# A tuned skewness kernel rewritten as one hand-synchronised section: x in a ring of two blocks, the transposes in a loop on PE, one ACT sum in every block

## The chip, the cores and the metric

The kernel runs on one core of one Trainium2 chip. The metric is the device time in microseconds (us), as a median of several executions. The engines are called as in the profile: PE (matmuls), PEld (PE's weight loads, which lie beside its matmuls), DVE (vector), ACT (scalar), POOL (GpSimd), SP (SyncE, which here issues every load). Blocks, loads and pieces are numbered from 0, so the eight blocks are 0 to 7. "b2" is block 2.

## The reference

The input is 1024 rows of 8192 float32 values (33.5 MB); the output is the skewness of each row.

```python
mean = np.mean(x, axis=-1, keepdims=True)
std = np.std(x, axis=-1, keepdims=True)
z = (x - mean) / (std + 1e-8)
return np.mean(z ** 3, axis=-1)
```

## The kernel before

The rows lie in eight blocks of 128. Of each piece of a block, ACT makes the squares (and their sum), DVE multiplies the squares by x (and sums the cubes), and PE sums x itself: it transposes 128 columns at a time and lets the transposes add up in `tp`. ACT copies `tp` to SBUF, a small matmul by 1/n gives the mean, and a few small instructions close the block. Only in blocks 0 to 2 does ACT take 1024 columns of the plain sum off PE.

```python
UNITS = [                       # columns of each load, block by block
    [4096, 4096], [4096, 4096], [4096, 4096], [4096, 4096],
    [3584, 2304, 2304],
    [2304, 2304, 2048, 1536],
    [1664, 1792, 1920, 1664, 1152],
    [1024, 1024, 1152, 1280, 1408, 1152, 1152],
]
S1_ACT = {(0, 0): 1024, (1, 0): 1024, (2, 0): 1024}
X_BUFS = 8
# ... cut ...
for b, widths in enumerate(UNITS):
    tp = psum.tile([P, P], FP, tag="tp", name=f"tp_{b}")
    for k, w in enumerate(widths):
        xt = xpool.tile([P, w], FP, tag="x", name=f"x_{b}_{k}")
        nc.sync.dma_start(out=xt, in_=xv[b, :, c0 : c0 + w])
        for s, e in _slices(w):
            # ACT: square with sum of squares;  DVE: cube with sum of cubes
            # ... cut ...
        w_act = S1_ACT.get((b, k), 0)
        if w_act:               # ACT: sum of 1024 columns
            # ... cut ...
        for c in range((w - w_act) // P):
            nc.tensor.matmul(out=tp, lhsT=xt[:, c * P : (c + 1) * P], rhs=ident,
                             start=..., stop=..., is_transpose=True)
    nc.scalar.copy(out=tsb, in_=tp)
    nc.tensor.matmul(out=s1ps[:, b : b + 1], lhsT=tsb, rhs=onesn, start=True, stop=True)
```

A scheduling layer places the buffers and semaphores. Each PE instruction waits for the load that it reads.

## Time and profile before

| | before |
|---|---|
| time, median of 4 executions beside the changed kernel | 91.49 us (91.40 to 91.57) |
| span of the profiled execution | 89.7 us |
| busy: DVE, ACT, PE | 72.7, 72.1, 64.9 us |
| mean granted clock of PE | 0.978 |
| last landing of x | 83.56 us |

The span runs from the first to the last record of the profile; the time contains 1.8 us more. The prediction below shows the chain, the DMA strips and the end. Two more views of before matter for what came. The first is the view of waits. Each line names an engine, the tile and line that waited, what it waited for, then the total in us, the number of waits, and the longest.

```profile
PE tp L165 <- DMA x<-in_x_dram: 17.2, 14, 8.2
DVE sq L152 <- ACT sq L147: 13.3, 7, 9.2
...
ACT sq L147 <- DMA x<-in_x_dram: 9.9, 8, 6.0
...
ACT tsb L174 <- PE tp L165: 2.0, 2, 1.5
```

Everybody waits for x, ACT too: eight times, 5.95 us of it for the first load. ACT waits for PE's transposes at the copy into `tsb` only twice. The second is the strips of the page (the profile's summary): busy tenths and granted clock in 40 slices.

```profile
PE   0003999892882919989998988888987798969710
...
ACT  6003999699991999859898989978979898999950
...
PEclk9999999999999997599999999999999999999998
```

PE's clock falls once before the end, in slices 15 and 16, to half (34.6 to 38.0 us). There, 32 transposes take 5.38 us; ACT's copy waits 1.48 us for them, and nothing comes of it: at 43.61 us ACT waits for a load again.

### The profile page before, as it was taken

What the parts mean: (1) busy time and instruction counts of PE and PEld (TensorE: products, weight loads), DVE (VectorE), ACT (ScalarE), POOL (GpSimd) and SP (SyncE); (2) the same over time, 40 slices, a digit from 0 to 9 for tenths busy, and PEclk for the clock granted to TensorE, in tenths of its full rate; (3) what the DMA queues carried; (4) which work ended last, traced back from release to release, by engine and by line L of the source; (5) the groups of instructions that cost most, each with busy time, mean ns of one, the idle gap of its engine ahead of it and who ended that gap; (6) DMA issues with size and microseconds to landing.
All of it is one profiled execution on the core that took longest, in us unless ns stands there. A gap on an engine that the chain in (4) does not pass through costs nothing.

```text
span 89.7 us, 1368 instructions
## 1 busy us (share of the span) xinstructions
PE 64.9 (72%) x504; PEld 59.3 (66%) x504; DVE 72.7 (81%) x80; ACT 72.1 (80%) x106; POOL 11.3 (13%) x14
## 2 busy tenths in 40 slices
PE   0003999892882919989998988888987798969710
PEld 0003999791872909979897977877876787848500
DVE  1000498989999298995999999999999999999970
ACT  6003999699991999859898989978979898999950
POOL 3000000000000000000000000000005999900030
PEclk9999999999999997599999999999999999999998
DMA  3999999999999999999999999999999999994000
GB/s 117 351 424 438 424 431 431 431 431 424 446 416 431 424 438 424 424 438 427 415 409 418 419 427 419 421 415 419 409 414 417 404 413 411 421 412 161 0 0 2
DMA packets 4038, 33.64 MB, mean 375 GB/s; under 512 B 576, under 2 KB 576, under 8 KB 2240
## 3 DMA queue, kind: packets, MB, share of 16 engines
q1 hardware_dynamic: 4032, 33.56, 89.7%
q8 instruction: 4, 0.07, 0.3%
q14 instruction: 2, 0.02, 0.0%
HBM read 33.55 MB, written 0.00 MB: 374 GB/s over the span
## 4 chain that ended last, share of the span: by engine, by line
DMA 73%; ACT 13%; issue 5%; DVE 4%; SPq 1%; PE 1%; DVEq 0%; ACTq 0%
DMA x<-in_x_dram 73%; ACT sq L147 9%; DVE sq L152 3%; ACT sqps L147 1%; ACT same L159 1%; SPq L140 1%; PE s1ps L175 1%; ACT tsb L174 0%; ACT s3u L128 0%; ACT v L127 0%; ACT var L125 0%; DVE num L189 0%; ACT m1sq L124 0%; DVE skew L192 0%; ACT nm L126 0%
## 5 line engine op out<-in xcount | busy, mean ns | idle before, releaser
L152 DVE SCALAR_TENSOR_TENSOR sq<-sq,x 128x2048 f32<-128x2048 f32 (+9 forms) x35 | 70.7, 2071 | 13.4 <-ACT sq L147 13.3
L165 PE MATMUL tp<-ident,x 128*128 128x128 f32 x488 | 62.6, 288 | 17.3 <-DMA x<-in_x_dram 17.2
L165 PEld LDWEIGHTS tp<-ident,x 128*128 128x128 f32 x488 | 57.9, 150 | 20.9 <-DMA x<-in_x_dram 12.7
L147 ACT ACTIVATE sq<-x 128x2048 f32<-128x2048 f32 (+9 forms) x35 | 60.6, 1734 | 10.7 <-DMA x<-in_x_dram 9.9
L110 POOL TENSOR_TENSOR vara<-m2a,m1sqa 128x6 f32<-128x6 f32 x1 | 1.8, 1822 | 67.1 <-DVE m3a L99 67.1
L147 ACT ACTIVATION_READ_ACCUMULATOR sq<-x 128x1 f32 x35 | 6.5, 186 | 0.0
L175 PEld LDWEIGHTS s1ps<-onesn,tsb 128*128 128x128 f32 x16 | 2.4, 188 | 5.2 <-ACT tsb L174 5.2
L175 PE MATMUL s1ps<-onesn,tsb 128*128 128x1 f32 x16 | 3.1, 260 | 3.3 <-ACT tsb L174 3.3
L174 ACT COPY tsb<-tp 128x128 f32<-128x128 f32 x8 | 2.0, 256 | 2.0 <-PE tp L165 2.0
L114 POOL TENSOR_TENSOR rra<-vara,expo 128x6 f32<-128x6 f32 x1 | 3.3, 3267 | 0.0
L159 ACT ACTIVATE same<-x 128x1024 f32<-128x1024 f32 x3 | 3.1, 1041 | 0.0
L152 DVE DVE_READ_ACCUMULATOR sq<-sq,x 128x1 f32 x35 | 2.9, 83 | 0.0
L111 POOL TENSOR_TENSOR m1sq3a<-m1sq3a,vara 128x6 f32<-128x6 f32 x1 | 1.9, 1868 | 0.1
L77 ACT ACT_TABLE_LOAD x1 | 1.3, 1283 | 0.7 <-PEq L208 0.7
L187 POOL TENSOR_TENSOR rr<-var,expo 128x2 f32<-128x2 f32 x1 | 0.7, 702 | 7.7 <-ACT var L125 7.7
L152 DVE SCALAR_TENSOR_TENSOR cube<-sqps,x 128x1152 f32<-128x1152 f32 x1 | 1.4, 1350 | 0.0
L113 POOL TENSOR_TENSOR m3a<-m3a,m1sq3a 128x6 f32<-128x6 f32 x1 | 1.2, 1201 | 0.1
L147 ACT ACTIVATE sqps<-x 128x1152 f32<-128x1152 f32 x1 | 1.1, 1136 | 0.1
L115 POOL TENSOR_TENSOR skew<-m3a,rra 128x6 f32<-128x6 f32 x1 | 1.1, 1069 | 0.1
L124 ACT ACTIVATE m1sq<-s1ps 128x1 f32<-128x1 f32 x2 | 0.3, 171 | 0.5 <-PE s1ps L175 0.5
L75 DVE MEMSET onesn<- 128x1 f32 x1 | 0.1, 59 | 0.8 <-PEq L208 0.8
L112 POOL TENSOR_TENSOR m1sq3a<-m1sq3a,nm1a 128x6 f32<-128x6 f32 x1 | 0.7, 697 | 0.0
(28 smaller groups left out, 6.8 us busy)
## 6 DMA issues: line engine op xcount, KB each, us to landing
x<-in_x_dram SPq DMA_DIRECT2D x8, 2048.0 KB, 23.4
x<-in_x_dram SPq DMA_DIRECT2D x4, 1152.0 KB, 27.9
x<-in_x_dram SPq DMA_DIRECT2D x4, 576.0 KB, 8.6
x<-in_x_dram SPq DMA_DIRECT2D x1, 1792.0 KB, 33.0
x<-in_x_dram SPq DMA_DIRECT2D x2, 832.0 KB, 13.9
x<-in_x_dram SPq DMA_DIRECT2D x1, 1024.0 KB, 21.1
x<-in_x_dram SPq DMA_DIRECT2D x2, 512.0 KB, 10.0
x<-in_x_dram SPq DMA_DIRECT2D x1, 960.0 KB, 13.2
```

The costliest lines, as they stand in the source:

```text
L77: nc.scalar.activation(out=tiny, in_=onesn, func=AF.Square)
L110: g.tensor_tensor(out=var, in0=m2, in1=m1sq, op=ALU.subtract)
L111: g.tensor_tensor(out=m1sq3, in0=m1sq3, in1=var, op=ALU.add)
L113: g.tensor_tensor(out=m3, in0=m3, in1=m1sq3, op=ALU.add)
L114: g.tensor_tensor(out=rr, in0=var, in1=expo, op=ALU.pow)
L115: g.tensor_tensor(out=skew[:, 0:F], in0=m3, in1=rr, op=ALU.mult)
L147: nc.scalar.activation(out=sq, in_=xt[:, s:e], func=AF.Square, scale=s_scale, accum_out=s2u[:, j : j + 1],)
L152: nc.vector.scalar_tensor_tensor(out=cube, in0=sq, scalar=1.0, in1=xt[:, s:e], op0=ALU.mult, op1=ALU.mult, accum_out=s3u[:, j : j + 1],)
L159: nc.scalar.activation(out=same[:, 0:w_act], in_=xt[:, w - w_act : w], func=AF.Copy, scale=inv_n, accum_out=s1a[:, b : b + 1],)
L165: nc.tensor.matmul(out=tp, lhsT=xt[:, c * P : (c + 1) * P], rhs=ident, start=(k == 0 and c == 0), stop=(c0 == C and c == n - 1), is_transp ...
L174: nc.scalar.copy(out=tsb, in_=tp)
L175: nc.tensor.matmul(out=s1ps[:, b : b + 1], lhsT=tsb, rhs=onesn, start=True, stop=True)
```

## The change

The intent was to make PE's program small enough (56 transposes a block, two blocks in a loop of four trips) that its instruction packets vanish (before has four of 16 KB on queue 8, 1.02 to 1.09 us each), to halve the memory for x, and to cut the number of loads from 27 to 24. The whole program is now one section whose semaphores are placed by hand. The core of the diff, with cuts at "...":

```diff
-    [3584, 2304, 2304],
-    [2304, 2304, 2048, 1536],
-    [1664, 1792, 1920, 1664, 1152],
-    [1024, 1024, 1152, 1280, 1408, 1152, 1152],
+    [2304, 2944, 2944],
+    [2176, 1664, 2176, 2176],
+    [1920, 2304, 2304, 1664],
+    [1536, 1920, 1792, 1664, 1280],
 ]
-S1_ACT = {(0, 0): 1024, (1, 0): 1024, (2, 0): 1024}
-X_BUFS = 8
+S1_ACT = 1024
+RING = 2
+ISSUE_LAG = 6500
+PARTS = (
+    [2048, 4096, 6144, 7168, 8192],
+    [2048, 4096, 5120, 6144, 7168, 7680, 8192],
+)
 ...
+    ring = sb("ring", RING * C)
 ...
+    ready = []
+    for u, (b, k, s, e) in enumerate(units):
+        free = []
+        if b >= RING:
+            o = b - RING
+            free = [("cube", max(i for i in of_block[o] if slices[i][2] < e)),
+                    ("part", o, min(i for i, p in enumerate(PARTS[o % RING]) if p >= e)),
+                    ("s1a", o)]
+        ready.append((max(b * C + e - RING * C + ISSUE_LAG, 0) if b >= RING else 0, u, 0, free))
+        n = sum(s < p <= e for p in PARTS[b % RING])
+        if n:
+            ready.append((b * C + e + 900, u, n, [("x", u)]))
+    for _, u, n, waits in sorted(ready, key=lambda r: r[:2]):
+        if n:
+            pr.op("sync", ("more", u), waits, lambda n=n: nc.sync.sem_inc(more, n), counts=False)
+        else:
 ...                              # the load of unit u, behind its waits
+    def pe_program(tensor):
+        tensor.wait_ge(*pr.marks["ident"])
+        tensor.wait_ge(*pr.marks["onesn"])
 ...
+        with nc.Fori(0, NB // RING, engines=..., head_slot={only: 0}):
+            for h in range(RING):
+                c0 = S1_ACT
+                for i, end in enumerate(PARTS[h]):
+                    tensor.sem_inc(more, -1)._wait_ge(more, 1)
+                    for c in range(c0, end, P):
+                        t = nc.tensor.matmul(out=tp[h], lhsT=at(h, c, c + P), rhs=ident, ...)
```

The loop's body is the same code in each trip and names no load's own semaphore. So PE waits for one counter, `more`, and SP raises it when a load has landed. SP therefore has one ordered list with two kinds of entries: loads, each behind the waits that free its part of the ring, and releases of PE, each behind the landing that it reports. `ISSUE_LAG` sets where a load stands in that list.

## The prediction

> **What bounds the kernel now.** I read the page's chain of work first, then its strips of 40 slices and its DMA queues.

> ```profile
> DMA 73%; ACT 13%; issue 5%; DVE 4%; SPq 1%; PE 1%; DVEq 0%; ACTq 0%
> ...
> DMA  3999999999999999999999999999999999994000
> GB/s 117 351 424 438 424 431 431 431 431 424 446 416 431 424 438 424 424 438 427 415 409 418 419 427 419 421 415 419 409 414 417 404 413 411 421 412 161 0 0 2
> ...
> q8 instruction: 4, 0.07, 0.3%
> ```

> The load of x is the path: 73% of it, and all 16 DMA engines are at 9 from slice 1 to slice 35. A buffer that frees sooner or a faster DVE cannot move that. But the strip holds an oddity. Slice 36 (80.7 to 82.97 us) moves 161 GB/s, slice 37 nothing, and yet the last square waits for x until 83.56 us. So I asked for the end in short stretches (length, then busy time and count of PE, PEld, DVE, ACT, POOL, then clock, DMA share, GB/s):

> ```profile
> 80.00:81.00 1.00, 0.58 (x6) 0.35 (x5) 1.00 (x1) 1.00 (x3) 0.00 (x0) 1.00 1.07 423
> 81.00:81.50 0.50, 0.50 (x6) 0.50 (x6) 0.50 (x3) 0.50 (x1) 0.00 (x0) 1.00 0.64 258
> 81.50:82.00 0.50, 0.50 (x7) 0.50 (x5) 0.50 (x1) 0.50 (x1) 0.00 (x0) 1.00 0.32 129
> 82.00:82.50 0.50, 0.50 (x5) 0.27 (x4) 0.50 (x3) 0.50 (x3) 0.00 (x0) 1.00 0.18 74
> 82.50:83.00 0.50, 0.50 (x7) 0.50 (x6) 0.50 (x1) 0.50 (x1) 0.00 (x0) 1.00 0.11 46
> ```

> A share of 0.11 is two of sixteen engines. Two stragglers hold the end. In the trace's records of the last load's 16 landings, the median engine is done at 81.89 us and the last two at 83.41 and 83.56. In the first load the spread from median to last is only 0.45 us (7.64 to 8.09). So some 1.2 us of the end is skew that grew on the way. It grew in jumps, each at an instruction packet: queue 8 has 16 KB packets at 26.28, 47.37, 65.24 and 80.88 us, taking 1.02 to 1.09 us each. The load that lands after the first has one engine 1.2 us late (28.85 against a next-to-last 27.65); after the second there are two. PE has issued about 230, 470, 730 and 1000 matmuls and weight loads at these times, so these are PE's instructions[...].[...]

> The tail after the last landing, in order of time (start, duration, engine):

> ```profile
> 83.58 1.14 ACT L147 ACTIVATE sqps<-x 128x1152 f32<-128x1152 f32 x1
> ...
> 84.84 0.27 ACT L174 COPY tsb<-tp 128x128 f32<-128x128 f32 x1
> ...
> 85.58 0.17 ACT L124 ACTIVATE m1sq<-s1ps 128x1 f32<-128x1 f32 x1 [0.27 <-PE s1ps L175]
> ...
> 86.16 0.70 POOL L187 TENSOR_TENSOR rr<-var,expo 128x2 f32<-128x2 f32 x1 [7.68 <-ACT var L125]
> ...
> 87.04 0.16 DVE L192 TENSOR_TENSOR skew<-num,rr 128x2 f32<-128x2 f32 x1
> 87.23 0.35 SPq L193 DMA_DIRECT2D out_dram<-skew  x1
> ```

> The store is issued 3.67 us after the last landing; the span ends 2.47 us later, at 89.7, and the time adds 1.78 (91.48). ACT takes the last square the moment it lands: it has no backlog.

> [...]

> **The change, part by part.**

> *PE's loop.* Two blocks are 2 x 56 transposes, so 224 matmuls and loads, with 4 more for the means and some semaphore instructions: [...]the four 16 KB packets mostly vanish. I leave one for entry or exit[...]. The last landing should then trail the median by 0.5 to 0.6 us, not 1.67.

> *Fewer, larger loads late.* 24 loads for 27. An engine moves 8 rows of a load; row packets of 4096 bytes have a median of 163 ns and of 16384 bytes 611 ns, so about 14 ns of each does not scale. 3 x (8 x 14 + 9 for the semaphore) is 0.36 us per engine. Median end 81.89 - 0.36 = 81.5; last landing about 82.1. **The DMA ends 1.4 to 1.5 us earlier.**

> *The ring.* Two blocks, 64 KB per partition for eight buffers of 16 KB: half the lookahead. A reload of block b+2 goes out some 8 us after its piece landed (the lag of 6500 columns at 10 us a block), or when its cube is done, about 5 us; the slot is needed 20 us less one load's 3 to 5 us after. Some 7 us to spare: no starvation.

> *ACT.* Squares start 1.91 us apart at 2048 columns, 1.05 at 1024: 0.2 us and 0.83 ns a column. A sum of 1024 takes 1.04. Blocks 0 to 3 cost 4 x 1.91 + 1.04 + 0.25 (the copy) = 8.9 us, below the 10.0 that a block takes to arrive. But block 7, where before had no such sum, now carries five squares (1.48, 1.80, 1.70, 1.59, 1.27: 7.84), the sum (1.04), block 6's close (seven small instructions; from starts 0.1 to 0.35 apart, 1.3) and the copy: 10.4 us.

> *PE's grain.* When block 6's last load (1664 columns) lands, no part beyond column 6144 has been released, so 16 transposes remain. At 16 in 1.94 us (the matmuls at 75.40) that is 2.1 us with the hop through SP. In block 7 the same: 16 transposes after the last landing, where before had 9 (1.20 us).

> *The walk through the end.* Block 6 lands at 72.15. Its last square ends at 73.75, but the copy waits for PE until 74.25 and ends at 74.5. Block 7's first piece has been there since 74.05. From here ACT is bound by itself: +1.48 = 75.98, sum 77.02, second square 78.82, two steps of the close 79.27, third 80.97, two steps 81.32, fourth 82.91, two steps 83.21, fifth 84.48, last step 84.68. The last piece landed at 82.1 and PE finished at 84.2, so neither delays the copy at 84.7. Before had 0.74 us from copy to m1sq: 85.42; 0.58 to rr: 86.0; 0.70 and a hop: skew at 86.85. DVE: fourth cube 83.0 to 84.82, fifth to 86.35, reduce and the new multiply-add to 86.8. Store at about 87.05, for 87.23 before.

> **Sum:** DMA end -1.4 us; ACT's backlog at the end takes back about 1.2. Entry and exit of a hand-synchronised section: not known from this trace[...]. That gives 91.3; the close steps are my weakest term and their waits partly lie under the squares, so I shade to **91.1**.

> **The rivals.**
> *The whole DMA gain arrives.* If ACT has no backlog in block 7, the tail keeps about before's 3.7 us after 82.1, perhaps 0.4 more for PE's 16 transposes: 89.9 to 90.2 us. For it: the sizes look tuned for this tail. Against it: 10.4 us of ACT work in 10.1 us of arrivals, and a late start.
> *The loop stalls PE.* If a back edge costs some us of fetching, PE still has 10 - 56 x 0.12 = 3.3 us of slack per block, so the time hardly moves (91.3). If each back edge also refetches 16 KB through a loaded engine, the skew stays and ACT's backlog comes on top: 92.2.
> *Ring starvation.* A reload that waits behind SP's ordered list of releases and loads leaves holes in the DMA strip; a hole of 1 us in the last blocks gives 92 or more. Against it, the 7 us of slack.
> *Entry cost.* A barrier ahead of the first load would shift everything[...].

> **Range and chances.** Centre 91.1, 90.1 from the first rival, 92.0 from the others. Faster by over 2% needs below 89.65: earlier than even the first rival, so 0.06. Slower by over 2% needs above 93.3, several faults at once: 0.04.

> **What would show it.** Queue 8's instruction packets down from four to one or none; DMA share falling from full to nothing within about 0.6 us at the end; last landing near 82.1. ACT with no idle time between about 74.5 and 85, and its last square starting a microsecond after its data. PE idle before its last 16 transposes. No slice below 9 in the DMA strip. I am wrong if the skew survives without fetches, if the last square still waits for DMA, or if the first load starts late.

The sum came to 91.3 us (91.48 - 1.4 + 1.2) and was shaded to 91.1; the guess for entry and exit stood beside it and is cut, but was not in the 91.3. That the 16 KB packets would mostly vanish was my estimate: in before, PE's records up to each of the four packets are 232, 480, 745 and 954, so 209 to 265 from one to the next, and a trip of the loop has 232 (928 in four). The rival's fetch at each back edge was a conjecture, which e3 tests. The hop through SP inside the "2.1 us" was an estimate too. It was right: where PE waited for a landing, it started 0.17 us after it in the changed kernel (24.28 for 24.11), and 0.04 us after it in before (28.89 for 28.85).

## The result, and the profile after

The changed kernel is correct and takes **105.14 us** (median of 4, 104.62 to 105.38), before 91.49 in the same rounds: a ratio of 1.1485, with a 95% interval of 1.1441 to 1.1529. Ratios are the mean time of one kernel's fast runs over that of the other's of the same rounds, so not quite the ratio of the medians. All four executions of the changed kernel count as fast; PE's granted clock in them was 0.87 to 0.88.

The page of the changed kernel, in the lines that answer to those of before:

```profile
span 102.3 us, 1354 instructions
...
PEclk9999999999999655998558999985999996559985
DMA  4899999999999999999999999999999970000000
GB/s 102 359 429 423 429 423 448 429 416 435 435 435 429 416 435 423 420 422 428 428 404 430 417 405 294 283 360 359 410 427 432 424 313 4 0 0 0 0 0 2
...
q8 instruction: 1, 0.02, 0.1%
...
POOL 1%; ACT 1%; PE 0%; issue 0%; DVE 0%; DVEq 0%; POOLq 0%
```

The instruction packets did fall from four to one. But four slices (24 to 27, 61 to 72 us) move 283 to 360 GB/s for some 420: the loads were issued too late. PE's clock is at about half in five places. And the DMA ends in slice 33 while the span runs on to slice 39. The chain covers only the last 2 us of this kernel and stops there (why is not shown), so it can't be used as in before. The waits can:

```profile
PE tp L347 <- PEq L345: 25.9, 11, 9.6
DVE sq L192 <- ACT sq L183: 24.5, 13, 10.3
...
ACT tsb L209 <- PE tp L347: 10.1, 4, 4.6
...
ACT sq L183 <- DMA ring<-in_x_dram: 8.6, 3, 7.1
PE s1ps L335 <- PEq L334: 7.8, 5, 4.2
ACT m1sqa L228 <- DVE m1a L216: 2.7, 1, 2.7
```

ACT hardly waits for x any more (7.1 of the 8.6 us are the first load). It waits 10.1 us for PE's transposes, where before had 2.0, and 2.7 us for the means, which before did not. PE waits for its own sequencer, which sits at the counter `more`. So the question passes to SP, whose queue has its own view of waits:

```profile
SPq L319 <- DMA ring<-in_x_dram: 27.7, 9, 6.5
SPq L323 <- DVE sq L192: 17.7, 13, 1.9
SPq L71 <- PE tp L347: 15.0, 7, 3.8
...
SPq L71 <- ACT same L200: 11.3, 4, 4.7
```

Line 319 is the releases: they should wait for landings only. Line 323 and the helper's line 71 are loads that wait for a cube, for PE, or for ACT's sum two blocks back: 44 us in all. Each such wait also holds the releases behind it. In order of time, at block 2 (start, duration, engine, what; in brackets the idle time before and who ended it):

```profile
33.28 2.29 DVE L192 SCALAR_TENSOR_TENSOR sq<-sq,ring 128x2048 f32<-128x2048 f32 x1
...
33.92 1.91 ACT L183 ACTIVATE sq<-ring 128x2048 f32<-128x2048 f32 x1
35.49 0.08 DVE L192 DVE_READ_ACCUMULATOR sq<-sq,ring 128x1 f32 x1
...
35.60 6.91 SPq L323 DMA_DIRECT2D ring<-in_x_dram  x3
...
36.13 6.84 PE L347 MATMUL tp<-ident,ring 128*128 128x128 f32 x40 [4.15 <-PEq L345]
...
42.13 0.27 ACT L209 COPY tsb<-tp 128x128 f32<-128x128 f32 x1 [4.32 <-PE tp L347]
```

The second load of block 2 has landed: ACT squares it at 33.92. PE could start too. But its release stands in SP's list behind the first load of block 4, and that one waits for a cube of block 2 which ends at 35.49. SP issues the load at 35.60 and only then raises the counter; PE starts at 36.13. By now PE has been idle for 4.15 us, its clock has fallen to 0.5 (at 34.0), and 32 transposes take about 6 us where 3.7 is usual. ACT's copy waits 4.32 us, which delays the next squares, cubes, reloads and releases. At block 3 the same happens (PE idle 4.50 us, then 32 transposes in 6.15 us, ACT idle 4.57 us).

The list's keys show it without a trace. The load of columns 0 to 2304 of block 4 has the key 4 x 8192 + 2304 - 2 x 8192 + 6500 = 25188. The release of the second half of block 2 has 2 x 8192 + 8192 + 900 = 25476, so it stands behind. For block 5's first load and block 3's release the keys are 33252 and 33668. There is a third pair, block 6's last load (47460) before the release of block 5's third load (47876): the load waits for a cube that ends at 67.10 us, PE idles 1.86 us and starts at 67.66, and its clock falls at 68.1.

The end of the changed kernel, in the same form:

```profile
82.52 0.15 DVE L216 TENSOR_TENSOR m1a<-s1ps,s1a 128x2 f32<-128x2 f32 x1
...
82.70 0.21 ACT L228 ACTIVATE m1sqa<-m1a 128x6 f32<-128x6 f32 x1 [2.71 <-DVE m1a L216]
...
86.69 0.24 ACT L209 COPY tsb<-tp 128x128 f32<-128x128 f32 x1
...
87.07 0.56 PE L335 MATMUL s1ps<-onesn,tsb 128*128 128x1 f32 x2 [4.18 <-PEq L334]
...
97.06 0.24 ACT L209 COPY tsb<-tp 128x128 f32<-128x128 f32 x1
...
99.64 0.35 SPq L327 DMA_DIRECT2D out_dram<-skew  x1
```

The last landing is at 85.36 us, but ACT only enters block 7 after its copy at 86.69 and works 10.4 us to the last copy at 97.06. ACT's 2.71 us before the means are a wait of one in-order engine for another: DVE makes `m1a` behind a cube whose square ACT has just made. In short stretches (length, busy time of PE, PEld, DVE, ACT, POOL, clock, DMA share, GB/s), the DMA ends like this:

```profile
83.00:84.00 1.00, 0.00 (x0) 0.00 (x0) 0.00 (x0) 1.00 (x3) 0.70 (x4) 1.00 0.76 309
84.00:84.50 0.50, 0.00 (x0) 0.00 (x0) 0.00 (x0) 0.50 (x1) 0.50 (x2) 1.00 0.13 51
84.50:85.00 0.50, 0.00 (x0) 0.00 (x0) 0.00 (x0) 0.50 (x1) 0.50 (x1) 1.00 0.05 20
```

One straggling engine remains (0.05 is less than one of sixteen): last landing 85.36, median engine 84.24.

### A ledger of ACT

One way of reading made the runs add up. ACT's timeline is cut at two places: where it takes the first square of block 3 (A), and where its last copy into `tsb` starts (B). Between them I add the waits that the timeline shows in brackets; the rest I call work. From B to the span's end, and from the span to the measured time, are two remainders. So time = A + work + waits + two remainders, by construction, for the profiled execution of each kernel:

| kernel | A | work | waits: transposes, means, other | B | B to span end | beyond span | time |
|---|---|---|---|---|---|---|---|
| before | 39.37 | 42.52 | 0, 0, 2.95 | 84.84 | 4.86 | 1.80 | 91.50 |
| changed | 42.29 | 46.23 | 5.83, 2.71, 0 | 97.06 | 5.24 | 2.86 | 105.16 |
| e1 | 38.89 | 46.29 | 0.94, 2.71, 0 | 88.83 | 5.27 | 2.65 | 96.75 |
| e2 | 38.94 | 46.30 | 0.97, 2.70, 0 | 88.91 | 5.29 | 2.60 | 96.80 |
| e3 | 41.79 | 46.27 | 8.03, 2.70, 0 | 98.79 | 5.51 | 1.84 | 106.14 |
| e4 | 38.90 | 46.32 | 3.27, 2.70, 0 | 91.19 | 5.21 | 2.19 | 98.59 |
| e5 | 38.77 | 46.21 | 2.56, 0, 0 | 87.54 | 5.36 | 2.50 | 95.40 |
| e6 (wrong result) | 39.02 | 42.71 | 3.14, 2.71, 1.21 | 88.79 | 5.81 | 2.55 | 97.15 |
| e7 | 39.64 | 46.14 | 1.99, 2.71, 0 | 90.48 | 5.32 | 1.69 | 97.49 |
| e8 | 38.82 | 46.17 | 0.99, 0, 0 | 85.98 | 5.42 | 1.70 | 93.10 |
| e9 | 38.89 | 46.18 | 2.28, 0, 0 | 87.35 | 5.45 | 2.89 | 95.69 |
| e10 (wrong result) | 38.86 | 43.12 | 3.96, 0, 1.21 | 87.15 | 5.25 | 2.46 | 94.86 |
| e11 | 39.51 | 41.71 | 0, 0, 3.53 | 84.75 | 5.65 | 1.88 | 92.28 |
| e12 | 38.96 | 46.33 | 4.25, 2.71, 0 | 92.25 | 5.25 | 1.77 | 99.27 |
| e13 | 39.20 | 46.32 | 3.54, 2.70, 0 | 91.76 | 5.24 | 1.78 | 98.78 |
| e14 | 38.97 | 46.31 | 4.80, 0, 0 | 90.08 | 5.32 | 1.78 | 97.18 |
| e15 (wrong result) | 39.13 | 42.87 | 6.84, 0, 0.72 | 89.56 | 5.24 | 1.78 | 96.58 |
| e16 | 38.99 | 41.68 | 6.65, 0.36, 1.00 | 88.68 | 5.82 | 1.73 | 96.23 |
| e17 | 39.09 | 42.32 | 2.57, 0, 1.65 | 85.63 | 5.27 | 1.75 | 92.65 |
| e18 | 39.15 | 41.93 | 2.30, 1.22, 1.43 | 86.03 | 5.77 | 2.21 | 94.01 |

("Other" is waits for loads; in before also 0.56 for a cube and 0.74 for the means' matmul, in e11 also that 0.74. The ledger says where ACT's time went, not why.) Three things stand out. In every version that sums 1024 columns in each block, ACT's work is 46.1 to 46.3 us, 3.7 more than before. In all of them ACT waits for no load after A. So from block 3 on ACT has no slack: each microsecond that it waits for PE or DVE comes out at the end, as long as no wait for a load takes its place (none does down to e8, with 0.99 us of waits). And the 13.66 us of this pair are: A later by 2.92, work 3.71 more, waits 5.59 more (8.54 for 2.95), tail 0.38 more, beyond the span 1.06 more.

### The profile page after: what moved, and what is told of

Its sections match the earlier page's. It is cut to its first block, busy times and chain, and to the rows that moved or that the text cites. A ratio compares the mean times of both kernels' runs of the same rounds, so it can differ in the third digit from the quotient of the medians.

```text
span 102.3 us, 1354 instructions
## 1 busy us (share of the span) xinstructions
PE 64.0 (63%) x464; PEld 61.5 (60%) x464; DVE 73.6 (72%) x79; ACT 76.2 (74%) x112; POOL 5.9 (6%) x14
## 5 line engine op out<-in xcount | busy, mean ns | idle before, releaser
L192 DVE SCALAR_TENSOR_TENSOR sq<-sq,ring 128x2048 f32<-128x2048 f32 (+8 forms) x34 | 72.4, 2164 | 24.7 <-ACT sq L183 24.5
L347 PE MATMUL tp<-ident,ring 128*128 128x128 f32 x448 | 62.1, 307 | 25.9 <-PEq L345 25.9
L347 PEld LDWEIGHTS tp<-ident,ring 128*128 128x128 f32 x448 | 59.5, 162 | 27.4 <-issue 27.4
L183 ACT ACTIVATE sq<-ring 128x2048 f32<-128x2048 f32 (+8 forms) x34 | 61.2, 1803 | 8.6 <-DMA ring<-in_x_dram 8.6
L209 ACT COPY tsb<-tp 128x128 f32<-128x128 f32 x8 | 2.1, 260 | 10.1 <-PE tp L347 10.1
L200 ACT ACTIVATE same<-ring 128x1024 f32<-128x1024 f32 x8 | 8.4, 1044 | 0.0
L183 ACT ACTIVATION_READ_ACCUMULATOR sq<-ring 128x1 f32 x34 | 6.4, 187 | 0.0
L235 POOL TENSOR_TENSOR vara<-m2a,m1sqa 128x6 f32<-128x6 f32 x1 | 0.2, 198 | 81.3 <-ACT m1sq3a L229 81.3
L192 DVE DVE_READ_ACCUMULATOR sq<-sq,ring 128x1 f32 x34 | 2.8, 83 | 0.0
L200 ACT ACTIVATION_READ_ACCUMULATOR same<-ring 128x1 f32 x8 | 1.5, 188 | 0.0
L235 POOL TENSOR_TENSOR rra<-vara,expo 128x6 f32<-128x6 f32 x1 | 1.3, 1336 | 0.0
```

What stands on the lines that cost most here:

```text
L183: pr.op("act", ("sq", i), waits, lambda: act(out=sqs[i % SQ_BUFS][:, 0 : e - s], in_=at(b, s, e), func=AF.Square, scale=s_scale, accum_out ...
L192: pr.op("dve", ("cube", i), [("sq", i), "s3u"], lambda: dve.scalar_tensor_tensor(out=sq, in0=sq, scalar=1.0, in1=at(b, s, e), op0=ALU.mult ...
L200: pr.op("act", ("s1a", b), us + prev, lambda: act(out=same, in_=at(b, 0, S1_ACT), func=AF.Copy, scale=inv_n, accum_out=s1a[:, b : b + 1],))
L209: lambda: nc.scalar.copy(out=tsb[b % RING], in_=tp[b % RING]).then_inc(copied, 1),
L235: pr.op("pool", name, waits, lambda: g.tensor_tensor(out=out, in0=in0, in1=in1, op=op))
L347: t = nc.tensor.matmul(out=tp[h], lhsT=at(h, c, c + P), rhs=ident, start=c == S1_ACT, stop=c + P == C, is_transpose=True,)
```

## The experiments

Four kinds of theory were on the table: that the order of SP's list holds PE back (A); that the small ring (B) or the loads' sizes hold up the DMA; that the loop itself stalls PE (C); and that ACT's wait for the means (D) and its sums (E) fill ACT up. F (the fetch at the loop's entry) and G (PE's clock) came later. Runs of one look have one time, with before on the same chip at 91.50 to 91.66. The state of a single run is unknown; e17, timed four times, scatters by 2.05 us. So the large differences (e1, e3, e12) carry the argument, and one of 1 to 2 us between single runs only where the ledger shows which wait has gone.

### e1: move three reloads behind the releases that they held

```diff
-ISSUE_LAG = 6500
+ISSUE_LAG = 7000
```

> One number changed: the lag that places each reload in SP's list, 6500 to 7000 columns, so that the reload of block 4's first piece comes behind the release of block 2's second half, and the first reload of block 5 behind the release of block 3's second half. Theory A (SP's list: a release of PE is stuck behind a reload that waits for a cube): PE starts its second half of block 2 at about 34.0 us instead of 36.1 and that of block 3 at about 43.8 instead of 49.4, ACT no longer waits 4.3 and 4.6 us for its copy, time 92 to 97 us (later releases may still be stuck). Theory B (the ring of two blocks is too small): reloads come no earlier, time within 2 us of 105. Theory C (PE's loop stalls at its back edge): unchanged, 105.

Measured: 96.75 us, clock 0.945. One number takes 8.4 us off. The keys of the three loads become 25688, 33752 and 47960 and now stand behind the releases (25476, 33668 and 47876); nothing else in the list changes places. (The text on record names two of the three.) PE's timeline at the same two places, and one later:

```profile
34.14 3.68 PE L347 MATMUL tp<-ident,ring 128*128 128x128 f32 x32 [2.09 <-PEq L345]
...
43.93 3.68 PE L347 MATMUL tp<-ident,ring 128*128 128x128 f32 x32 [1.91 <-PEq L345]
...
61.07 5.45 PE L347 MATMUL tp<-ident,ring 128*128 128x128 f32 x48 [2.61 <-PEq L345]
```

PE starts block 2's second half at 34.14 for 36.13, idles about 2 us instead of 4, keeps its full clock, and 32 transposes take 3.68 us. The hole in the DMA strip is gone. In the ledger, A is 3.40 earlier and the waits for transposes 4.89 shorter: 8.29 of the 8.41 us. The order of the list is the main cause. The kernel is still 5.1 us slower than before.

### e2: reloads later still

```diff
-ISSUE_LAG = 6500
+ISSUE_LAG = 8500
```

> The same number at 8500 columns: all reloads come about 2.4 us later in the list than in the changed kernel. Theory A: no release is stuck behind a reload, PE starts within 0.3 us of each landing, its clock is granted at 1.0 but for at most one dip, time 91 to 95 us. Theory B: reloads issued later starve DMA more, 105 or slower. Theory C: unchanged, 105.

Measured: 96.80 us, the same as e1, so the expectation (91 to 95) was too low. SP's waits for DVE halve (20.0 us in e1, 9.9 here) and nothing follows. Once the releases are free of the loads' waits, what SP still waits for costs nothing, and the ring of two blocks is large enough. Something else holds the remaining 5 us. All later versions with "lag" have this value.

### e3: the loop written out

```diff
-        with nc.Fori(0, NB // RING, engines=bass.OrderedEngineSet([only]), head_slot={only: 0}):
+        for trip in range(NB // RING):
```

> PE's loop undone alone: the same 464 matmuls in the same order with the same waits, written out. Theory A and B: 104 to 106 us, with queue 8's instruction packets back at three or four. Theory C (the loop's back edges stall PE): PE's waits of 4 us go, time below 97.

Measured: 106.14 us, no faster. The transposes have 13.2 us of ACT's waits (10.1 with the loop), so the loop is not the cause; C falls. Written out, PE has three instruction packets again, and at 72.8 us, beside the packet of 72.17, it stands still for 1.82 us. With the loop's packet gone from the first load, the first square starts at 8.36 us (9.46 with the loop), and that gain is lost later.

### e4: a ring of four blocks, unrolled, the list's order as it was

```diff
+XRING = 4
-    ring = sb("ring", RING * C)
+    ring = sb("ring", XRING * C)
-        if b >= RING:
-            o = b - RING
+        if b >= XRING:
+            o = b - XRING
```

(and the loop written out, so that PE can address four blocks.)

> Ring of four blocks instead of two (PE's loop written out for it), SP's list in exactly the order of the changed kernel: a reload stands at the same place but the cube, transposes and sum that it waits for are two blocks older and long done. Theory A: nothing in the list blocks any more, 91 to 95 us. Theory B: also recovers, as the buffers are there, 91 to 95; so this run does not tell A from B, it shows that the wait of a reload is the cause in either case. If the cause lies in PE's clock or in ACT's extra sums alone: 100 or more.

Measured: 98.59 us; expected 91 to 95, a miss. A reload now finds its part of the ring free, SP waits only 0.9 us for cubes, and A is 38.90 as in e1. So the *waits* of the reloads hold the releases, not the place in the list as such. The miss is in part PE's: it stands still for 2.10 us at 64.9 to 67.0, beside an instruction packet at 64.70, and ACT's copy waits 2.48 us, at full clock (before the end it falls at 39.2 and at 80.2 us only). The means' 2.70 stay.

### e5 and e9: the means before the cube

```diff
-ISSUE_LAG = 6500
+ISSUE_LAG = 8500
+        pos = i - of_block[b][0]
         square(i)
+        if b and b % RING == 0 and pos == 1 and b <= F:
+            means(b // RING - 1)
         cube(i)
-        pos = i - of_block[b][0]
 ...
-        if b and b % RING == 0 and pos == 1 and b <= F:
-            means(b // RING - 1)
```

> Lag 8500, and DVE adds the means of the early blocks before the cube of the second slice instead of after it. Theory D (ACT's three early steps in block 6 wait for a DVE instruction queued behind the cube of the very slice that ACT has just squared): ACT's idle 2.7 us in front of m1sqa goes to under 0.3 us; ACT then may wait up to 1 us for PE at block 6's copy; time 94.0 to 95.3 us, for 96.8 without it. Rival (ACT has slack there, the tail is set elsewhere): 96.5 or more.

> The kernel of e5 again, timed: lag 8500 and means early. Theory G (what still scatters is PE's granted clock: after a gap PE runs a window of about 3.4 us at half rate, and ACT's in-order copy waits for it): the executions differ by more than 1 us among each other and the slower ones have the lower mean clock; those near 0.99 take 93 to 94 us, those near 0.93 take 95 to 96. Rival (clock does not matter, e8 was faster for its waits in the loop): all executions within 0.5 us of 95.4 whatever their clock.

Measured: 95.40 us in one look; the same kernel timed: 95.66 us (95.24 to 95.69, four executions), ratio to before 1.0439 (1.0411 to 1.0468). Both lie just above what D expected for e5 (94.0 to 95.3). ACT's wait of 2.7 us for the means is gone from the list of waits, but only 1.1 to 1.4 us of it came out of the time: ACT now waits 2.56 (2.28) us for transposes instead of 0.97. Spread between executions was under half a microsecond, so the scatter that I thought of is not in this kernel. By the text the rival came true (all within 0.5 us of 95.4, at clocks of 0.920 to 0.954); whether its reason does, the waits in the loop, is taken up at e8.

### e6: a sum of 128 columns

From e2, with a wrong result:

```diff
-            out=same, in_=at(b, 0, S1_ACT), func=AF.Copy, scale=inv_n, accum_out=s1a[:, b : b + 1],
+            out=same[:, 0:P], in_=at(b, 0, P), func=AF.Copy, scale=inv_n, accum_out=s1a[:, b : b + 1],
```

> Lag 8500, and ACT's sum of every block over 128 columns instead of 1024: a WRONG result on purpose, to take away 0.75 of its 1.04 us per block. Theory E (from block 4 on ACT is the bound and the added sums are on the path): about 4 x 0.75 = 3 us, time 93.0 to 94.5 us. Rival (ACT is held by PE's copies and by the wait for the means, the sums fill idle time): gain under 1 us, 96 or more.

Measured: 97.15 us, where 93 to 94.5 was expected; that is in the range of the rival. ACT's work fell by 3.6 us, as reckoned. The waits rose by 3.4. From the view of waits:

```profile
ACT sq L183 <- DMA ring<-in_x_dram: 12.8, 9, 7.2
...
ACT tsb L209 <- PE tp L347: 3.1, 2, 2.2
ACT m1sqa L228 <- DVE m1a L216: 2.7, 1, 2.7
```

With less to do, ACT reaches its copies sooner and waits there for PE (3.14 after A, for 0.97 in e2), and for loads (1.21). PE comes to its 48 transposes of block 5 no sooner, and here its clock fell (60.6 to 64.0 us). So taking work off ACT alone turned into waiting; the expectation had counted the sums as if PE were far ahead.

### e7: PE's two constant waits inside the loop

From e2:

```diff
     def pe_program(tensor):
-        tensor.wait_ge(*pr.marks["ident"])
-        tensor.wait_ge(*pr.marks["onesn"])
 ...
         with nc.Fori(...):
+            tensor.wait_ge(*pr.marks["ident"])
+            tensor.wait_ge(*pr.marks["onesn"])
```

> Lag 8500, and PE's two waits for the constants moved from ahead of the loop into it, so that PE branches into the loop before the loads start. Theory F (entering the loop fetches one 16 KB packet at 5.8 us behind the first load on one engine, which makes every landing 1.2 us late): queue 8's packet starts before 2.5 us, the first square at 8.3 to 8.5 us instead of 9.5, the last landing trails the median by under 0.7 us instead of 1.5; time 95.3 to 96.0 us. Rival (the packet is fetched for another reason or is queued anyway): packet stays near 6 us and time 96.8.

Measured: 97.49 us (expected 95.3 to 96). The aim was to get PE's one instruction packet, at the loop's entry, out of the first load. It moved from about 5.8 to 3.9 us, still inside that load, and the first square still waited 7.1 us. The ledger shows something that I had not looked for: "beyond span" fell from 2.60 to 1.69. The other entries gave back more: A is 0.70 later, the waits for transposes 1.02 longer, at a clock of 0.913.

### e8: lag, means and waits in the loop together

From e5:

```diff
-        tensor.wait_ge(*pr.marks["ident"])
-        tensor.wait_ge(*pr.marks["onesn"])
 ...
         with nc.Fori(...):
+            tensor.wait_ge(*pr.marks["ident"])
+            tensor.wait_ge(*pr.marks["onesn"])
```

> Lag 8500, means early and waits in the loop together. If D and F add: 92.5 to 94.3 us. If ACT's work from block 4 on bounds it whatever comes earlier (theory E): 94 or more.

Measured: **93.10 us**, the best with all the sums; one execution. The clock was 0.997: no fall before the end. The lines of PE at block 5, from e5 and from e8:

```profile
60.96 7.07 PE L347 MATMUL tp<-ident,ring 128*128 128x128 f32 x48 [2.62 <-PEq L345]
```

```profile
61.04 5.45 PE L346 MATMUL tp<-ident,ring 128*128 128x128 f32 x48 [2.62 <-PEq L344]
```

```profile
57.49:60.90 3.41, 0.85 (x9) 0.77 (x7) 2.94 (x5) 3.41 (x6) 0.00 (x0) 1.00 1.01 424
60.90:64.31 3.41, 3.35 (x16) 3.38 (x17) 3.13 (x5) 3.41 (x5) 0.00 (x0) 0.50 1.01 421
```

```profile
56.71:60.12 3.41, 1.71 (x17) 1.63 (x15) 2.89 (x5) 2.65 (x4) 0.00 (x0) 1.00 1.00 419
60.12:63.53 3.41, 2.49 (x23) 2.52 (x24) 3.23 (x3) 3.41 (x5) 0.00 (x0) 1.00 1.02 424
```

In e5 one stretch holds nearly the whole gap; in e8 a line of the grid cuts the gap in two. The 20 traces, with the grid carried back from the recorded changes, have 419 such stretches at full clock, from the clock's first record on (14.14 us in before). The clock fell after 47 of them, each with PE's matmuls busy for less than 0.46 of the stretch; of the 372 others none lies below 0.43. (In before and the changed kernel alone: seven falls, each after a share of 0.46 or less; the lowest share without one is 0.47.) So in these runs the fall goes with the share of a stretch, not with the length of one gap: in e1 the clock fell at 70.0 us, and the longest gap in the stretch before was 1.51 us. Where the grid lies changes from run to run: e5 and e9 are the same kernel, and it lies 0.5 us apart in them. The waits in the loop do not prevent the fall: e7 has them, and its clock fell three times before the end. Of the 2.30 us by which e8 is below e5, 1.57 are waits for transposes, 0.80 lie beyond the span; the other entries differ by 0.1 at most. Its ledger is nearly bare: 46.17 us of work, 0.99 of waits.

### e10: means early and narrow sum

From e5, with e6's edit:

```diff
-            out=same, in_=at(b, 0, S1_ACT), ...
+            out=same[:, 0:P], in_=at(b, 0, P), ...
```

> Lag 8500, means early and ACT's sums over 128 columns (a WRONG result on purpose). With the wait for the means gone, theory E (the added sums lie on ACT's path from block 4 on) says 91.0 to 93.0 us where no PE clock dip falls into block 5 to 7, and ACT waiting for DMA again in the last blocks. Rival (PE's copies bind, sums fill idle time): as e5, 94.5 to 95.5.

Measured: 94.86 us. The time is in the rival's range (94.5 to 95.5). The clock fell three times before the end; ACT waited 6.0 us for transposes over the whole run. The ledger has 3.1 us less work than e5 and 2.6 us more waits. As a measure of the sums' cost it is inconclusive; as a second sight of e6 it agrees.

### e11: before, with only the new sizes of loads

```diff
-    [3584, 2304, 2304],
-    [2304, 2304, 2048, 1536],
-    [1664, 1792, 1920, 1664, 1152],
-    [1024, 1024, 1152, 1280, 1408, 1152, 1152],
+    [2304, 2944, 2944],
+    [2176, 1664, 2176, 2176],
+    [1920, 2304, 2304, 1664],
+    [1536, 1920, 1792, 1664, 1280],
```

> The kernel before with nothing but the new load sizes of blocks 4 to 7 (24 loads for 27). If the sizes were a cause of the loss: over 93 us. My theory (the sizes alone are nearly free; 3 loads fewer save about 0.3 us of DMA, a longer last load costs a little): 91.0 to 92.0 us.

Measured: 92.23 us (92.15 to 92.29), ratio 1.0077 (1.006 to 1.0094), just above the expected 91.0 to 92.0: the sizes alone cost 0.7 us. By the ledger they lie behind the last copy (5.65 us to the span's end, for 4.86).

### e12: full clock by force, the list untouched

From e3 (unrolled, lag 6500), with extra matmuls that nobody reads:

```diff
+        def keep_warm(n):
+            for _ in range(n):
+                nc.tensor.matmul(out=filler, lhsT=ident, rhs=fill, start=True, stop=True)
 ...
                 for i, end in enumerate(PARTS[h]):
+                    keep_warm({0: 1, 2: 3}.get(i, 0) if trip or h else 0)
```

> The changed kernel with PE's loop written out (as e3, 106.1 us) and SP's list untouched, but PE runs filler matmuls (three of 512 columns before the wait for each block's third part, one before its first) into an unused bank, so that its clock is not lowered in the gaps. Theory G as amplifier: the late releases stay, but the 40 and 32 transposes after them take 4.6 and 3.7 us instead of 7.5 and 6.5, ACT's waits for the copies shrink from 13 us to under 7, time 98 to 102 us. Rival (the late release alone is the loss): 105 or more.

Measured: 99.27 us, within the expected 98 to 102. The clock strips of e3 and of e12:

```profile
PEclk9999999999999556996559975999999999589955
```

```profile
PEclk9999999999999999999999999999999999999995
```

At nearly full clock (0.990, for 0.877 in e3), with SP's list in the same wrong order, 6.9 us go. So here the fall of the clock multiplied the late releases: they were the trigger (the lag alone, e1, takes off 8.4 us), and half speed made most of the damage. (e1's 8.4 and these 6.9 overlap; they don't add. The 6.9 are net of what the extra matmuls cost, which the next runs show to be something.)

### e13, e14, e15: the fixes on top of the forced clock

Each builds on the one before: e13 on e12, e14 on e13, e15 (wrong) on e14.

```diff
 e13:
-ISSUE_LAG = 6500
+ISSUE_LAG = 8500
 e14:
         square(i)
+        if b and b % RING == 0 and pos == 1 and b <= F:
+            means(b // RING - 1)
         cube(i)
 e15:
-            out=same, in_=at(b, 0, S1_ACT), ...
+            out=same[:, 0:P], in_=at(b, 0, P), ...
```

> e12 (PE written out, filler matmuls) with lag 8500. With the clock held, the list order alone should be worth what ACT waits for its copies after blocks 2 to 5 in e12 (2.0, 1.4, 0.8 us and less): 95.0 to 96.5 us, for 99.3 in e12, with ACT's waits for the copies below 1.5 us in all and the 2.7 us for the means still there. If the order matters only through the clock: 98.5 or more.

> e13 with the means added before the second slice's cube: the 2.7 us wait goes, 92.4 to 93.7 us (e8, which had no clock dip by luck, took 93.1). If the waits in the loop were what made e8 fast: 94.5 or more.

> e14 with ACT's sums over 128 columns, a WRONG result on purpose. Theory E (sums on ACT's path from about block 4 on): 2 to 3 us less than e14, 90.3 to 91.5 us, ACT waiting for DMA again in the last blocks. Rival (something else bounds the tail): less than 0.7 us off e14.

Measured: 98.78, 97.18 and 96.58 us; expected 95 to 96.5, 92.4 to 93.7 and 90.3 to 91.5. All three missed, in the same direction. My own tool was the bound: each block now holds some 3.8 us of extra matmuls beside 6.4 to 6.7 us of transposes, and PE can't go far into the next block before ACT's copy. In e13 PE takes 21.06 us for two blocks (48.85 to 69.91), more than the 20 in which they arrive. So these runs decide little: all three lie in the ranges of their rivals (98.5 or more, "only through the clock"; 94.5 or more, the waits in the loop; less than 0.7 us off e14), but the bound of the tool explains that as well. In e14 ACT waits 4.80 us for transposes at a full clock; in e15 3.4 us of work went and 2.8 us of waits came.

### e16: sums in blocks 0 to 2 only, old sizes, forced clock

From e14, with two extra matmuls instead of three ahead of the third part:

```diff
-    [2304, 2944, 2944],          (and the next three blocks)
+    [3584, 2304, 2304],
     def first_sum(b):
+        if b >= 3:
+            return
 ...
-                c0 = S1_ACT
+                c0 = first = S1_ACT if trip * RING + h < 3 else 0
```

> The hand-synchronised section with all repairs, ACT's sums only in blocks 0 to 2 as before (PE does 64 transposes from block 3 on), the load sizes of before, two filler matmuls instead of three: right result. If list order, means, clock and sums are the whole loss, it equals the kernel before: 91.0 to 92.2 us. If the hand-made synchronisation itself costs: 93 or more.

Measured: 96.18 us (96.10 to 96.23), ratio 1.0501; expected 91 to 92.2. ACT's work is near that of before (41.68 for 42.52), but it waits 6.65 us for PE, which from block 3 on has 64 transposes a block and the extra matmuls as well. This is the same fault of the experiment as in e13 to e15.

### e17 and e18: few sums without extra matmuls

e17 is e5, unrolled, with the sums in blocks 0 to 2 only; e18 is e17 with the old sizes.

```diff
 e17:
     def first_sum(b):
+        if b >= 3:
+            return
 ...
-        with nc.Fori(0, NB // RING, ...):
+        for trip in range(NB // RING):
 ...
-                c0 = S1_ACT
+                c0 = first = S1_ACT if trip * RING + h < 3 else 0
 e18:
-    [2304, 2944, 2944],          (and the next three blocks)
+    [3584, 2304, 2304],
```

> Lag 8500, means early, ACT's sums in blocks 0 to 2 only (PE written out, 64 transposes from block 3 on), no fillers, the new load sizes, right result. Theory E (the sums in blocks 3 to 7, 5.2 us of ACT's time, are what kept e5 and e9 at 95.5): 91.8 to 93.5 us. Rival (PE's clock or PE's coupling with ACT's copies bounds it, and PE has more to do now): 94.5 or more, with ACT's waits for its copies at 3 us or more.

> e17 with the load sizes of the kernel before. If list order, means and sums are the whole loss and the hand-made section is free: 91.0 to 92.3 us, 0.3 to 1 us below e17 (the sizes alone cost the kernel before 0.7). If the section itself costs (entry, SP's posting of releases, PE's stalls on fetching): 93 or more.

Measured, e17: 92.65 and 92.63 us in its two fast executions (clock 0.970, 0.964); 94.13 and 94.68 in two that count as slow by the rule (more than 1.5% above the fastest; clock 0.953, 0.952). The fast two lie in what E expected (91.8 to 93.5). e18: 94.46 us (94.01 to 95.06), ratio 1.0323 (1.0275 to 1.0372), expected 91 to 92.3.

e17's fast executions are 3.0 us below e9, whose sums and loop they lack. In the ledger 3.9 us less work, 1.9 more waits and 1.1 less beyond the span. ACT waits for loads again (1.65 us after A), as in before. Against before, 1.15 us are left: 1.27 more waits, 0.4 behind the last copy, less 0.5 elsewhere. These 2.57 us of waits for transposes are what before doesn't have:

```profile
PE tp L353 <- PEq L351: 22.4, 10, 8.3
...
ACT tsb L215 <- PE tp L353: 4.6, 5, 1.6
```

e18 undoes one more part and is not faster: 94.01 to 95.06, beside e17's fast pair at 92.6 and its slow pair at 94.1 and 94.7, so whether it is slower is not clear. The sizes' 0.7 us, found in before, are not regained; the waits for the means come back (1.22). e18 lies in the range of its rival (93 or more, the section itself costs), which is not excluded. What the last one to three microseconds are made of stays open.

No version with a right result beats before.

## Why the prediction was wrong

It said 91.1 us, within 90.1 to 92.0; the kernel took 105.14. Point by point, in its own steps:

**"The ring": the step that failed.** The prediction put it: "Some 7 us to spare: no starvation." It asked when a slot is needed by the DMA, and for that question it was right: with the list in order (e1, e2) the strip has no hole and more waiting room brings nothing. It did not ask who else stands in SP's list. A reload that waits for a cube with 7 us to spare is harmless; a release of PE behind it has no microsecond to spare. The rival "ring starvation" did name "SP's ordered list of releases and loads", but only as a source of holes in the DMA strip, sized 1 us. The harm went to PE first, at 34 us, and the holes came at 61 us. In its place: three loads in front of three releases, 8.4 us (e1).

**"3.3 us of slack per block" on PE.** The 0.12 us of a transpose in it holds only at full clock. At half clock it is 0.17 to 0.19 us (40 in 6.84 us, 32 in 6.15 us), and 56 would take 10 us (an estimate from these). Against e1 the release at block 2 came 2.0 us later (36.13 for 34.14) and the copy 4.3 us later (42.13 for 37.86), so the slower transposes added 2.3. e12 puts the clock's part of the whole at about 6.9 us. The one dip in before's strip was in front of me and I passed over it as harmless, as in before it was.

**"ACT. ... 8.9 us, below the 10.0 that a block takes to arrive" and the walk.** The sizes were right. Block 7's work was predicted as 10.4 us and took 10.4 in the changed kernel (86.69 to 97.06) and in e8 (75.61 to 85.98). Even the end was nearly right: A of 38.85 and 46.2 us of work without waits give 85.05 us for the last copy (an estimate from the ledger), for 84.7 predicted. But the walk let ACT be free until block 6 ("From here ACT is bound by itself"). It is bound from block 3: in e1 the second load of block 3 lands at 43.76 and ACT is free for it only at 43.79, and block 4's first lands at 46.55 and is taken at 47.82. So waits of PE and DVE that before absorbed in its 2.95 us of idle time come straight out at the end here. The walk counted one of 0.5 us; e1 still has 3.65.

**The means.** The walk has no wait of ACT for DVE's `m1a`. It is 2.71 us in every version that keeps its place, and moving it took 1.1 to 1.4 us off (e2 to e5 and e9). Missed altogether.

**"DMA end -1.4 us".** Failed, though its means held: packets within the span fell from four to one. That one falls at the loop's entry, 5.73 us, into the first load: its last engine lands at 9.43 us against a median of 7.9. The last landing then trails to the end: in e1 83.46 us against a median of 82.0; before had 83.56 against 81.89. "It grew in jumps, each at an instruction packet" misread this: in before the trail is 1.65 us after the first packet (28.85 against 27.20) and still 1.67 at the end. The later packets added next to nothing, so here one packet early cost what four did. The prediction had left one packet "for entry or exit" without asking when.

**"Entry and exit ... not known from this trace".** The first load goes out at 0.96 us for 0.74: 0.22. But another 0.7 to 1.1 us lie beyond the span in all seven profiled executions that have the loop with the two waits ahead of it (2.46 to 2.89 us), and in neither kernel with the waits inside (1.69, 1.70); without the loop it is 1.73 to 2.21. The packed traces show a reason: in all seven a second 16 KB instruction packet of queue 8 starts 1.73 to 1.94 us after the span's last record, and the time ends with it (the packets end 2.66 to 3.10 us after the span, and in each of the seven the time ends about 0.2 us before that); e7 and e8 have none. So queue 8 still carried two packets, one at the loop's entry and one after the end, where the prediction left one "for entry or exit".

**Right:** three back edges cost nothing that can be seen (e3 is no faster, though it has a stall of 1.82 us of its own), and PE's transposes fit once they start in time. **Sizes: small, but the wrong way.** The fewer loads end the DMA's median 0.21 us earlier (e11: 81.68 for 81.89; predicted 0.36), and the kernel takes 0.7 longer.

**The account.** Of 13.7 us, the list's order explains 8.4 (e1, shown by one number). Then the means take 1.1 to 1.4. e8 takes 2.3 more: 0.8 beyond the span, as in e7 (0.9), and 1.6 because the clock didn't fall, which hangs on where the grid lay; it is one execution. The 1.6 us between e8 and before are, in the ledger, 3.65 us more work of ACT less 1.96 us of waits, and small remainders. Most of this work is the five added sums: without them it is 3.9 us less (e17 for e9; by their own row they are 5 x 1.04 = 5.2 us). What they cost in time by themselves was not isolated, since each try (e6, e10, e15) let PE become the next bound, and e17 also writes the loop out.

## What to carry to other kernels

An engine's in-order list that carries both "tell the other engine to go" and "wait until a buffer is free" makes each message wait for buffers (here 8.4 us, e1): place messages ahead of such waits, or on another queue, and check it by comparing the sort keys. Reckon PE's slack at half clock (here 0.17 to 0.19 us a transpose for 0.12) if PE may be busy for as little of the time before a burst as here: all 47 falls came after 3.41 us with PE busy for less than 0.46. And before you call a wait absorbed, look whether the engine that waits still idles for data afterwards: where it didn't, from block 3 on here, each wait was added to the end (changed: 8.54 us of waits for 2.95).
